# Plain products in the first two feed-forward blocks of a two-layer encoder

## Chip, cores, metric

One core of one Trainium2 chip runs the whole program. The metric is device time of one execution in microseconds (us).

## The reference, cut to what matters

Two layers work on a residual x of 1024 prompt and 64 sample rows, width 1024. Each layer is a mixer followed by a SwiGLU feed-forward, both behind an RMS norm with a shift and scale from a conditioning vector:

```python
def rms_norm(x, g):
    xf = x.astype(f32)
    return xf * lax.rsqrt(jnp.mean(xf * xf, -1, keepdims=True) + EPS) * g.astype(f32)
...
        hn = (rms_norm(x, norm_ffn[l]) * (1.0 + sc2) + sh2).astype(x.dtype)
        x = x + ((1.0 + g2) * swiglu(hn, ffn_wg[l], ffn_wu[l], ffn_wd[l])).astype(x.dtype)
```

swiglu is silu(hn times gate matrix) times (hn times up matrix), times the down matrix; the hidden width D_FF is 2816, that is 22 blocks of 128.

## The kernel before

x lies transposed in eight tiles of 128 x 1088 (features by rows). Every fp32 product is three passes over operands that are split in a high part (a cast on ACT) and a low part (a subtraction on POOL or DVE, `split`, L98 and L99): high by high, high by low, low by high.

The up half of the feed-forward (`up_half`) goes over 22 blocks of 128 hidden features. The two matrices of a block (gate and up) and the two halves of the rows form a 2 x 2 problem, solved with seven products in place of eight. Each product is 2 x 12 matmuls of 272 columns, so a block has 168 matmuls, into four accumulators accX, accY, accZ, accW in PSUM. For this the normalised x is turned into seven operands (`ops`: some are x itself, some sums and differences of quarters of x), and the four weight quarters of a block into seven weights (`weights`, three of them sums), each split into wh (ACT) and wl (POOL) in rings of 5 buffers of 128 x 512.

The last out-projection of the mixer (`project`) goes over four chunks of 272 rows (CH4). After each chunk `enter` stores x to DRAM, takes the norm's sums (L223), the power -1/2 on POOL (L232), spreads it over the partitions by a matmul (L239), copies it to SBUF (L374), multiplies x by it (L376), applies scale and shift (L379), and after every second chunk makes the first four operands (`first_ops`). `late_ops` makes the other three at the start of `up_half`. Block 0 needs the first operands of both halves.

The down half (`down_half`) multiplies 22 hidden blocks, parked in DRAM (hid_dram), by w_down in eight groups of two or three blocks. x is loaded back from DRAM ahead of it (`unpark`). In layer 0 the conditioning of layer 1 is worked out during the down half: `ada_tick` is called after each of the 24 chunks of a group and does two or three column blocks, each two dot products (L191 to L194) on DVE, or one on DVE and one on POOL with ACT.

A scheduler writes each engine's instruction list out ahead of time; at run time each engine goes through its list in order. Pools hand out buffers in turn, and whoever takes a buffer waits for its last reader.

Of the kernel before, what the change touches and what calls it, by code (L numbers as in the profile page):

```python
# [21 lines left out]
KD = 8  # L22
# [32 lines left out]
def hybrid_encoder(ctx: ExitStack, tc: tile.TileContext, I, O):  # L55
# [20 lines left out]
    def soon():  # L76
        return tc.high_priority(offset=SOON)
# [7 lines left out]
    def psum_pool(name):  # L85
        stack = ExitStack()
        stage["psum"] = stack.enter_context(tc.tile_pool(name=name, bufs=1, space=bass.MemoryType.PSUM,
                                                         reuse_waits="tile"))
        return stack
# [235 lines left out]
    def split_at(src, dst, j, lo_eng):  # L325
        c = slice(j * Q, (j + 1) * Q)
        split(src, dst[:, 0, c], dst[:, 1, c], lo_eng)
# [4 lines left out]
    def enter(l, x, tag, stat_tmp, tmp):  # L332


        ops = [[] for _ in range(7)]

        def late_ops(j):
            A, B = slice(j * Q, (j + 1) * Q), slice(HT + j * Q, HT + (j + 1) * Q)
            for k in range(4):
                split_at(x[k + 4][:, A], ops[4][k], j, G)  # L340
            for k in range(4):
                V.tensor_sub(x[k + 4][:, A], x[k + 4][:, A], x[k][:, A])
                split_at(x[k + 4][:, A], ops[5][k], j, V)
            for k in range(4):
                d, c = x[k + 4][:, B], slice(j * Q, (j + 1) * Q)
                hi, lo = ops[6][k][:, 0, c], ops[6][k][:, 1, c]
                S.activation(hi, d, AF.Copy, scale=-1.0)
                V.scalar_tensor_tensor(lo, d, -1.0, hi.bitcast(F32), ALU.mult, ALU.subtract)

        def first_ops(j):  # L350
            A, B = slice(j * Q, (j + 1) * Q), slice(HT + j * Q, HT + (j + 1) * Q)
            if j == 0:
                for o, t in ((0, tag), (1, tag), (2, "C"), (3, "C")):
                    ops[o] = [halves(u(t, F32R, "op")) for _ in range(4)]
            for k in range(4):
                split_at(x[k][:, A], ops[0][k], j, V)
            for k in range(4):
                a, b, d = x[k][:, A], x[k][:, B], x[k + 4][:, B]
                t1 = tmp()[:, :Q]
                V.tensor_sub(t1, b, a)  # L360
                V.tensor_sub(b, b, d)
                V.tensor_sub(a, a, b)
                split_at(a, ops[1][k], j, V)
                split_at(b, ops[2][k], j, G)
                split_at(t1, ops[3][k], j, G)

        def after(ci):
            c0, n = CH4[ci]
            r = slice(c0, c0 + n)
            for k in range(KD):  # L370
                dma(x_dram[k][:, r], x[k][:, r])
            rs = norm_stats(CH4[ci], x, stat_tmp)
            kept = tmp()[:, :n]
            S.copy(kept, rs)  # L374
            for k in range(KD):
                (G if k in (2, 3, 7) else V).tensor_mul(x[k][:, r], x[k][:, r], kept)  # L376
                for r0, rn, b in rng(c0, n):
                    v = x[k][:, r0:r0 + rn]
# [4 lines left out]
        return (ops, late_ops), after  # L383

    def up_half(l, ops_late, t_tag, op_tag):
        ops, late_ops = ops_late
        with phase_pool(f"up{l}") as fp:
            layout(fp, ("n22", NT, 4), ("t4", NT, 4), ("b21", NT, 4), ("wg", 1024, 2), ("wu", 1024, 2), ("s1", 512, 1),
                   ("wh", 512, 5), ("wl", 512, 5))

            def w_split(src):
                hi = fp.tile([P, 512], F32R, name="wh", tag="wh", bufs=5)
                lo = fp.tile([P, 512], F32R, name="wl", tag="wl", bufs=5)
                split(src, hi, lo, G)
                return hi, lo

            def weights(f):
# [3 lines left out]
                dma(wu, I["wu"][l, f])  # L401
                s1 = fp.tile([P, 512], F32, name="s1", tag="s1", bufs=1)
                w11, w12, w21, w22 = wg[:, :512], wg[:, 512:], wu[:, :512], wu[:, 512:]
                with soon():
                    yield w_split(w11)
                    V.tensor_add(s1, w21, w22)
                    V.tensor_add(w21, w11, w21)
                    V.tensor_add(w11, s1, w11)
                    yield w_split(w11)
                    yield w_split(w21)  # L410
                    yield w_split(s1)
                    yield w_split(w12)
                    V.tensor_add(w12, w11, w12)  # L413
                    yield w_split(w22)
                    yield w_split(w12)

            with soon():
                for o, tag in ((4, "b21"), (5, "t4"), (6, "n22")):
                    ops[o] = [halves(fp.tile([P, NT], F32R, name="op", tag=tag, bufs=4)) for _ in range(4)]
                late_ops(0)  # L420
                late_ops(1)
            stage["open"].close()
            with psum_pool(f"acc{l}"):
                ap = stage["psum"]

# [9 lines left out]
                for f in range(FF):  # L435
                    X, Y, Z, W = (ap.tile([P, 2, 512], F32, name="acc" + n, tag="acc" + n, bufs=1) for n in "XYZW")
# [33 lines left out]
                    for part in ((steps[:4], steps[4:]) if f == 0 else [[st] for st in steps]):  # L470
                        wt = [next(ws) for _ in part]
                        for j in range(2):
                            for w, (acc, op, start, use) in zip(wt, part):
                                product(acc, w, op, j, start)
                                if j == 1:
                                    with soon():
                                        use()
# [13 lines left out]
    def down_half(l, x, fp, t_tag, after=None, last=None, tick=None):  # L491
        f = 0
        for gi, size in enumerate(GROUPS):
            hs, ws = [], []
            for f in range(f, f + size):
# [11 lines left out]
            f += 1  # L507
            if gi == len(GROUPS) - 1 and last:
                last(ws, hs)
            else:  # L510
                project(ws, hs, x, mod(l, 5), after if gi == len(GROUPS) - 1 else tick, ("t", "z", "mm"))

# [7 lines left out]
    with phase_pool("wp") as stage["w"], phase_pool("mix") as mp:  # L520
# [474 lines left out]
        def out_group(g, after=None, chunks=CH):  # L995
# [13 lines left out]
            project(ws, hs, x, mod(0, 2), after, ("t", "z") if after else ("mm", "mm"), chunks)  # L1009
# [40 lines left out]
        ops, after = enter(0, x, "A", slots(mp, "kv", 3, 2, 4), slots(mp, "wt", 2, 2, 3))  # L1050
# [27 lines left out]
    up_half(0, ops, "B", "A")  # L1078
    with phase_pool("ffn0") as fp:
# [3 lines left out]
        x = unpark("A")  # L1083
# [5 lines left out]
        def ada_tick(ci):  # L1089
            with later():  # L1090
                for n in range(3 if len(todo) > 24 else 2):
                    if not todo:
# [5 lines left out]
                             lambda: fp.tile([P, 1024], BF16, name="junk", tag="junk"), j % 2 == 0)  # L1098
# [3 lines left out]
        box2, after = norm_into(1, 0, "B", "C", x, ntmp, ntmp)  # L1102
        with later():
            decay_consts()
        down_half(0, x, fp, "B", after, tick=ada_tick)
# [3 lines left out]
    h = box2[0]  # L1109
    with phase_pool("odd") as gp, phase_pool("w2") as w2, phase_pool("wp2") as stage["w"]:  # L1110
# [99 lines left out]
        def odd_out(js, own, aft=None, chunks=CH):  # L1210
# [15 lines left out]
            project(ws, hs, x, mod(1, 2), aft, ("t", "z", "mm"), chunks)  # L1226
# [3 lines left out]
        ops, after = enter(1, x, "B", slots(gp, "un", 12, 2, 4, Q), slots(gp, "un", 12, 2, 4, Q))  # L1230
# [41 lines left out]
    up_half(1, ops, "A", "B")  # L1272
    with phase_pool("ffn1") as fp:
# [4 lines left out]
        def finish(ws, hs):  # L1278
# [116 lines left out]
        x = unpark("B")  # L1395
        down_half(1, x, fp, "A", last=finish)
# [75 lines left out]
```

## Time and profile before

| | before |
|---|---|
| median of three runs | 2861.4 us (2857.73 to 2866.29) |
| the profiled execution's own time | 2864.79 us |
| its span | 2863.0 us |
| mean granted TensorE clock | 0.946 |
| busy: PE, DVE, ACT, POOL | 2610.7, 1814.2, 1026.6, 1269.6 us |

The span is what the profile covers; the execution's own time is 1.8 us longer. PE is TensorE's matmuls, PEld its weight loads, SPq a DMA issue on SyncE. A busy share of PE counts overlapped matmuls once.

### The profile page before, as it was taken

Reading aid. Unit: us, or ns where it says so; the run is one execution under the profiler, and the core shown is the slowest. Engines: PE = TensorE matmul, PEld = TensorE weight load, DVE = VectorE, ACT = ScalarE, POOL = GpSimd, SP = SyncE. Lnnn points to the kernel's source line nnn. Section 1 sums busy time; section 2 is a strip of 40 time slices with the busy share of each in tenths; the row PEclk is TensorE's granted clock in tenths of the full one; section 3 lists DMA queues with packets and bytes.
Section 4 is the critical chain, followed back from the end, with each engine's and each line's share of the span. In section 5 each row is a group of like instructions: output and inputs, shape, how many; then the busy total and the mean of one; then the engine's idle time right before and its main releaser. Section 6 shows DMA issues by size and latency. Waiting matters only on the chain.

```text
span 2863.0 us, 44449 instructions
## 1 busy us (share of the span) xinstructions
PE 2610.7 (91%) x17584; PEld 2549.8 (89%) x17584; DVE 1814.2 (63%) x2806; ACT 1026.6 (36%) x1891; POOL 1269.6 (44%) x923
## 2 busy tenths in 40 slices
PE   6898999999894999999799969998769999989998
PEld 6898989998783999999799969998669999989997
DVE  8778664568988343443788875668864344346555
ACT  3224343353555322222422155563442222232112
POOL 6546443355636444444443453344454444433222
PEclk9999988999996999999899979999889999999998
DMA  6232112112211222222854411221212222253211
GB/s 235 89 115 87 55 45 80 43 62 105 71 62 63 69 83 77 70 89 63 291 171 161 133 62 55 67 68 51 92 38 81 78 69 91 68 177 130 94 43 63
DMA packets 104561, 260.93 MB, mean 91 GB/s; under 512 B 17185, under 2 KB 42785, under 8 KB 104353
## 3 DMA queue, kind: packets, MB, share of 16 engines
q1 hardware_dynamic: 104352, 258.10, 27.7%
q8 instruction: 138, 2.26, 0.3%
q14 instruction: 71, 0.57, 0.1%
HBM read 207.36 MB, written 50.69 MB: 90 GB/s over the span
## 4 chain that ended last, share of the span: by engine, by line
PE 60%; DVE 22%; DMA 5%; ACT 5%; issue 4%; POOL 4%; SPq 0%; DVEq 0%; POOLq 0%; ACTq 0%
PE accZ L431 9%; PE accX L431 9%; PE accW L431 9%; PE ps_mm L127 7%; PE ps_mm L311 5%; PE accY L431 5%; PE ps_t L311 4%; PE ps_z L311 4%; DVE junk L194 3%; DVE x L316 3%; DVE xc L51 2%; DMA w_raw<-in_adaT 1%; DVE om L779 1%; PE ps_z L882 1%; PE ps_z L770 1%
## 5 line engine op out<-in xcount | busy, mean ns | idle before, releaser
L99 POOL TENSOR_TENSOR w_lo<-w_raw,w_hi 128x1024 fp32r<-128x1024 f32 x88 | 236.1, 2692 | 377.0 <-ACT w_hi L98 333.5
L99 POOL TENSOR_TENSOR wl<-wg,wh 128x512 fp32r<-128x512 f32 x176 | 228.3, 1297 | 225.8 <-ACT wh L98 225.1
L431 PE MATMUL accX<-op,wh 128*128 128x272 f32 x1408 | 275.0, 291 | 33.6 <-ACT wh L98 33.6
L446 DVE TENSOR_TENSOR tg<-accY,tg 128x544 f32<-128x544 f32 x44 | 31.9, 724 | 386.2 <-PE accY L431 364.9
L431 PE MATMUL accW<-op,wh 128*128 128x272 f32 x1408 | 274.4, 287 | 0.0
L431 PE MATMUL accZ<-op,wh 128*128 128x272 f32 x1408 | 271.1, 287 | 0.0
L431 PEld LDWEIGHTS accX<-op,wh 128*128 128x128 f32 x1408 | 224.1, 191 | 34.2 <-ACT wh L98 34.2
L127 PE MATMUL ps_mm<-h_hi,w_hi 128*128 128x384 f32 (+1 forms) x640 | 219.6, 343 | 11.2 <-ACT w_hi L98 9.9
L431 PEld LDWEIGHTS accW<-op,wh 128*128 128x128 f32 x1408 | 223.2, 188 | 0.4 <-ACT wh L98 0.4
L431 PEld LDWEIGHTS accZ<-op,wh 128*128 128x128 f32 x1408 | 220.8, 188 | 0.4 <-ACT wh L98 0.4
L127 PE MATMUL ps_mm<-h_hi,w_lo 128*128 128x384 f32 (+1 forms) x640 | 218.0, 342 | 2.0 <-POOL w_lo L99 2.0
L127 PE MATMUL ps_mm<-h_lo,w_hi 128*128 128x384 f32 (+1 forms) x640 | 217.7, 340 | 0.0
L431 PE MATMUL accX<-op,wl 128*128 128x272 f32 x704 | 204.9, 291 | 12.7 <-POOL wl L99 12.7
L98 ACT CAST wh<-wg 128x512 fp32r<-128x512 f32 x176 | 109.1, 621 | 283.8 <-DVE wg L413 142.4
L431 PE MATMUL accW<-op,wl 128*128 128x272 f32 x704 | 202.6, 288 | 0.0
L431 PE MATMUL accZ<-op,wl 128*128 128x272 f32 x704 | 202.4, 288 | 0.0
L98 ACT CAST w_hi<-w_raw 128x1024 fp32r<-128x1024 f32 x86 | 88.8, 1049 | 244.3 <-PE ps_mm L311 164.0
L316 DVE SCALAR_TENSOR_TENSOR x<-ps_mm,mods,x 128x384 f32<-128x384 f32 (+4 forms) x306 | 140.2, 482 | 51.1 <-PE ps_mm L311 50.8
L99 POOL TENSOR_TENSOR wl<-wu,wh 128x512 fp32r<-128x512 f32 x88 | 132.7, 1508 | 56.4 <-ACT wh L98 46.4
L99 POOL TENSOR_TENSOR wl<-s,wh 128x512 fp32r<-128x512 f32 x44 | 56.9, 1293 | 213.9 <-ACT wh L98 203.2
L431 PEld LDWEIGHTS accX<-op,wl 128*128 128x128 f32 x704 | 134.5, 191 | 13.4 <-POOL wl L99 13.4
L431 PE MATMUL accY<-op,wh 128*128 128x272 f32 x704 | 137.4, 288 | 1.6 <-ACT wh L98 1.6
(464 smaller groups left out, 7992.7 us busy)
## 6 DMA issues: line engine op xcount, KB each, us to landing
ada_raw<-in_adaT SPq DMA_DIRECT2D x48, 512.0 KB, 3.5
hid_dram<-hid SPq DMA_DIRECT2D x88, 272.0 KB, 3.9
wg<-in_wg SPq DMA_DIRECT2D x44, 512.0 KB, 4.2
wu<-in_wu SPq DMA_DIRECT2D x44, 512.0 KB, 3.6
w_raw<-in_wd SPq DMA_DIRECT2D x44, 512.0 KB, 4.4
hid_lo<-hid_dram SPq DMA_DIRECT2D x40, 544.0 KB, 6.0
w_raw<-in_w_in_even SPq DMA_DIRECT2D x28, 512.0 KB, 3.6
w_raw<-in_adaT SPq DMA_DIRECT2D x24, 512.0 KB, 3.6
```

The source lines that it names most:

```text
L51: return lambda *a, **k: self.tc.keep_in_program_order(f(*a, **k))
L98: S.copy(hi, src)
L99: (lo_eng or G).tensor_sub(lo, src, hi.bitcast(F32))
L127: PE.matmul(ps[:, :n], a[:, k * P:(k + 1) * P], b[:, c0:c0 + n], start=(i == 0), stop=(i == last))
L194: V.scalar_tensor_tensor(junk(), raw, 1.0, cb[v], ALU.mult, ALU.mult, accum_out=mods[l][:, t, v:v + 1])
L311: PE.matmul(ps[:, :n], a[:, m * P:(m + 1) * P], b[:, c0:c0 + n], start=(i == 0), stop=(i == 3 * nk - 1))
L316: V.scalar_tensor_tensor(x[m][:, r0:r0 + rn], ps[:, r0 - c0:r0 - c0 + rn], gate[:, m, b:b + 1], x[m][:, r0:r0 + rn], ALU.mult, ALU.add)
L431: PE.matmul(acc[:, j, :Q], a[:, k * P:(k + 1) * P], op[k][:, b, c], start=(start == 1 and i == 0), stop=(i == 11), skip_group_check=True)
L446: V.tensor_sub(t, y_, t)
L770: PE.matmul(z[:M, :bn], qs[:, j, s * P:s * P + M], ks[:, k0 + b0:k0 + b0 + bn], start=(j == 0), stop=(j == 1))
L779: V.tensor_tensor_scan(om[:, 0:d][:, ::-1], om[:, 0:d][:, ::-1], om[:, 0:d][:, ::-1], om[:, d:d + 1], ALU.mult, ALU.bypass)
L882: PE.matmul(ps[:L, a, :L // 2], K[:, c0:c0 + L], q, start=True, stop=True)
```

## The change

- Blocks 0 and 1 of each layer take plain products (`plain_block`): per chunk of 272 rows two outputs of 24 matmuls, 192 a block, on operands that `enter` now writes directly (B11, B12, B21, B22, by L351 to L353 of the new file, which read the spread norm from PSUM). Blocks 2 to 21 keep the seven products; their operands are made by `sums` between the two plain blocks in program order.
- The rings of wh and wl have 6 buffers in place of 5. One weight sum is taken with the other sign.
- The PSUM banks are laid out in a fixed order; the last out-projection uses banks t and mm.
- The loads of x stand behind the loads of the first down group in program order.
- `ada_tick` does three column blocks each time until all 48 are done (16 ticks; before 20, three for 8 ticks and two for 12). Of 48 column blocks 30 share with POOL and ACT in place of 24.

```diff
-            kept = tmp()[:, :n]
-            S.copy(kept, rs)
+            o = c0 % HT
             for k in range(KD):
-                (G if k in (2, 3, 7) else V).tensor_mul(x[k][:, r], x[k][:, r], kept)
+                t = B[(1, 0, 2, 3)[2 * (k // 4) + ci % 2]][k % 4]
                 for r0, rn, b in rng(c0, n):
...
-                    S.activation(v, v, AF.Identity, scale=scale[l][1][:, k, b:b + 1], bias=mods[l][:, 3 * KD + k, b:b + 1])
-            if ci % 2:
-                first_ops(ci // 2)
...
+                    V.scalar_tensor_tensor(v, v, A, rs[:, r0 - c0:r0 - c0 + rn], ALU.mult, ALU.mult)
+                    S.activation(hi, v, AF.Identity, bias=bias)
+                    V.scalar_tensor_tensor(lo, v, bias, hi.bitcast(F32), ALU.add, ALU.subtract)
...
-                   ("wh", 512, 5), ("wl", 512, 5))
+            layout(fp, ("t4", NT, 4), ("t1", NT, 4), ("t3", NT, 4), ("wg", 1024, 2), ("wu", 1024, 2), ("s1", 512, 1),
+                   ("wh", 512, 6), ("wl", 512, 6), ("hid0", NT, 2))
...
+            def sums():
...
+                for k in range(KD):
+                    for r0, rn, b in rng(0, NT):
+                        v = x[k][:, r0:r0 + rn]
+                        S.activation(v, v, AF.Identity, bias=mods[l][:, 3 * KD + k, b:b + 1])
...
+                for k in range(4):
+                    a, b, c, d = x[k][:, :HT], x[k][:, HT:], x[k + 4][:, :HT], x[k + 4][:, HT:]
+                    V.tensor_sub(d, b, d)
+                    V.tensor_sub(b, b, a)
+                    V.tensor_sub(a, a, d)
+                    V.tensor_sub(c, c, a)
+                    split(d, T3[k][:, 0, :], T3[k][:, 1, :], V)
+                    split(b, T1[k][:, 0, :], T1[k][:, 1, :], G)
+                    split(c, T4[k][:, 0, :], T4[k][:, 1, :], G)
...
+                return B11, T2, T3, T1, B21, T4, B22
...
+                def plain_block(f, order):
+                    hid = fp.tile([P, NT], F32, name="hid0", tag="hid0", bufs=2)
+                    with soon():
+                        ws = [w_split(w) for w in fetch(f)]
+                    for n, ci in zip("XYZW", order):
...
+                        for v in range(2):
+                            i = 0
+                            for hf in range(2):
+                                op = ((B11, B21), (B12, B22))[ci % 2][hf]
+                                w = ws[2 * v + hf]
...
+                            S.activation(h, acc[:, 0, :Q], AF.Silu)
+                            V.tensor_mul(h, h, acc[:, 1, :Q])
...
+                plain_block(0, range(4))
+                ops = sums()
+                plain_block(1, (1, 3, 0, 2))
+                for f in range(2, FF):
...
+        got = fetch(0)
+        x = unpark(x_tag)
...
-                for n in range(3 if len(todo) > 24 else 2):
+                for n in range(3):
...
-                             lambda: fp.tile([P, 1024], BF16, name="junk", tag="junk"), j % 2 == 0)
+                             lambda: fp.tile([P, 1024], BF16, name="junk", tag="junk"), j % 3 != 0)
```

Three places of the instruction lists show where the change moves work. Numbers behind a name tell one buffer or tile from another; op is an operand, wh and wl a weight's high and low part.

First, PE where the up half of layer 0 begins. ps_o holds the norm's sums (L223, now L224) and its spread (L239, now L240) of chunks 2 and 3. Before:

```order
L223 MATMUL ps_o_8255<-ones_66,ntmp_7831 128x1 x3
L239 MATMUL ps_o_8262<-ident_65,r1_8259 128x128 x3
L431 MATMUL accX_8422<-op_7984,wh_8433 128x272 x2
L431 MATMUL accX_8422<-op_7984,wl_8434 128x272
```

Now:

```order
L224 MATMUL ps_o_8234<-ones_66,ntmp_7851 128x1 x3
L240 MATMUL ps_o_8241<-ident_65,r1_8238 128x128 x3
L435 MATMUL accX_8338<-op_7823,wh_8322 128x272 x2
L435 MATMUL accX_8338<-op_7823,wl_8323 128x272
```

The first product still stands behind the spread of the last chunk, but its operand op_7823 is one of the second chunk's, and its weight is w11 as loaded.

Second, POOL ahead of the weights of the first blocks in layer 0. Before, block 0's first wl stands behind the 16 operand splits of half 0 and 1:

```order
L99 TENSOR_TENSOR op_8352<-x_5909,op_8352 128x272
L99 TENSOR_TENSOR op_8353<-x_5910,op_8353 128x272
L99 TENSOR_TENSOR wl_8434<-wg_8428,wh_8433 128x512
L99 TENSOR_TENSOR wl_8441<-wg_8428,wh_8440 128x512
```

Now (wl_8331 and wl_8335 are block 0's, wl_8629 to wl_8641 block 1's, wl_8861 block 2's):

```order
L100 TENSOR_TENSOR wl_8335<-wu_8319,wh_8334 128x512
L100 TENSOR_TENSOR wl_8629<-wg_8624,wh_8628 128x512
L100 TENSOR_TENSOR wl_8633<-wg_8624,wh_8632 128x512
L100 TENSOR_TENSOR op_8559<-x_5907,op_8559 128x544
L100 TENSOR_TENSOR op_8560<-x_5908,op_8560 128x544
L100 TENSOR_TENSOR op_8567<-x_5911,op_8567 128x544
L100 TENSOR_TENSOR op_8561<-x_5909,op_8561 128x544
L100 TENSOR_TENSOR op_8568<-x_5912,op_8568 128x544
L100 TENSOR_TENSOR op_8562<-x_5910,op_8562 128x544
L100 TENSOR_TENSOR op_8569<-x_5913,op_8569 128x544
L100 TENSOR_TENSOR wl_8637<-wu_8625,wh_8636 128x512
L100 TENSOR_TENSOR op_8570<-x_5914,op_8570 128x544
```

Block 0's weights now stand ahead of all operand splits; the third weight of block 1 stands behind seven of them.

Third, PE in a seven-product block in mid-layer, at the second product into accX and accZ. Before:

```order
L431 MATMUL accW_10432<-op_8359,wh_10620 128x272
L431 MATMUL accX_10652<-op_8350,wh_10782 128x272 x2
L431 MATMUL accW_10432<-op_8359,wh_10620 128x272
L431 MATMUL accW_10432<-op_8359,wl_10621 128x272
L431 MATMUL accW_10432<-op_8360,wh_10620 128x272 x2
L431 MATMUL accW_10432<-op_8360,wl_10621 128x272
L431 MATMUL accW_10432<-op_8361,wh_10620 128x272 x2
L431 MATMUL accW_10432<-op_8361,wl_10621 128x272
L431 MATMUL accX_10652<-op_8350,wl_10783 128x272
```

Now:

```order
L449 MATMUL accZ_10635<-op_8566,wh_10705 128x272 x2
L449 MATMUL accZ_10635<-op_8566,wl_10706 128x272
L449 MATMUL accW_10190<-op_8560,wh_10288 128x272
L449 MATMUL accW_10190<-op_8560,wl_10289 128x272
L449 MATMUL accW_10190<-op_8561,wh_10288 128x272 x2
L449 MATMUL accW_10190<-op_8561,wl_10289 128x272
L449 MATMUL accW_10190<-op_8562,wh_10288 128x272 x2
L449 MATMUL accW_10190<-op_8562,wl_10289 128x272
L449 MATMUL accX_10633<-op_7827,wh_10763 128x272 x2
L449 MATMUL accZ_10635<-op_8567,wh_10793 128x272 x2
L449 MATMUL accX_10633<-op_7827,wl_10764 128x272
```

By the lists, wh_10763 goes into the buffer that wh_10705 leaves (the first row of this piece is its last reader), and wh_10793 into that of wh_10288, which accW of two blocks back still reads. Before, wh_10782 takes the buffer of a weight whose last matmul stands 26 matmuls ahead of its use.

## Rows read from the trace of the kernel before

**Rows 1.** The page: span, busy time by engine, chain that ended last.

```profile
span 2863.0 us, 44449 instructions
...
PE 2610.7 (91%) x17584; PEld 2549.8 (89%) x17584; DVE 1814.2 (63%) x2806; ACT 1026.6 (36%) x1891; POOL 1269.6 (44%) x923
...
PE 60%; DVE 22%; DMA 5%; ACT 5%; issue 4%; POOL 4%; SPq 0%; DVEq 0%; POOLq 0%; ACTq 0%
```

**Rows 2.** Windows: stretch, length, busy us by engine, granted clock, DMA.

```profile
940.00:1370.00 430.00, 430.00 (x3441) 430.00 (x3440) 182.46 (x226) 122.50 (x204) 191.79 (x143) 1.00 0.27 83
...
1400.00:1670.00 270.00, 260.63 (x1548) 256.92 (x1549) 241.44 (x419) 67.41 (x94) 120.80 (x52) 0.99 0.46 152
```

**Rows 3.** Windows of the transition into the up half, layer 0.

```profile
890.00:900.00 10.00, 0.00 (x0) 0.00 (x0) 9.86 (x19) 10.00 (x30) 5.66 (x7) 0.50 0.18 54
```

**Rows 4.** Timeline of PE there: start, us, operation, [idle before].

```profile
862.63 0.28 PE L311 MATMUL ps_z<-o_hi,w_lo 128*128 128x272 f32 x1
...
885.72 1.65 PE L239 MATMUL ps_o<-ident,r 128*128 128x128 f32 x6 [8.38 <-POOL r L232]
904.18 0.82 PE L431 MATMUL accX<-op,wh 128*128 128x272 f32 x2 [16.81 <-ACT wh L98]
911.38 0.59 PE L431 MATMUL accX<-op,wl 128*128 128x272 f32 x1 [6.37 <-POOL wl L99]
911.77 0.65 PE L431 MATMUL accX<-op,wh 128*128 128x272 f32 x2
```

**Rows 5.** Timeline of POOL there.

```profile
899.52 10.39 POOL L99 TENSOR_TENSOR op<-x,op 128x272 fp32r<-128x272 f32 x11
909.87 1.46 POOL L99 TENSOR_TENSOR wl<-wg,wh 128x512 fp32r<-128x512 f32 x1
```

**Rows 6.** Groups by form, 850 to 912 us: busy us, mean ns | idle before.

```profile
L99 POOL TENSOR_TENSOR op<-x,op 128x272 fp32r<-128x272 f32 x16 | 15.0, 959 | 0.0
...
L99 DVE TENSOR_TENSOR op<-x,op 128x272 fp32r<-128x272 f32 x16 | 11.1, 736 | 0.0
...
L259 DVE TENSOR_TENSOR ntmp<-ntmp 128x272 f32<-128x272 f32 x8 | 3.3, 428 | 0.0
...
L316 DVE SCALAR_TENSOR_TENSOR x<-ps_t,mods,x 128x272 f32<-128x272 f32 x3 | 1.5, 491 | 0.0
```

**Rows 7.** The chain of work, 938 to 1000 us: start, us, what.

```profile
948.49 3.01 PE accX L431 x24
```

**Rows 8.** Timeline in mid-layer, PE, ACT, POOL: one weight's hand-over.

```profile
1146.67 0.41 PE L431 MATMUL accX<-op,wh 128*128 128x272 f32 x2
...
1147.17 0.62 ACT L98 CAST wh<-s 128x512 fp32r<-128x512 f32 x1 [5.50 <-PE accX L431]
...
1147.87 1.29 POOL L99 TENSOR_TENSOR wl<-s,wh 128x512 fp32r<-128x512 f32 x1 [5.35 <-ACT wh L98]
```

**Rows 9.** The page's groups: weight loads of PE (mean ns).

```profile
L431 PEld LDWEIGHTS accX<-op,wh 128*128 128x128 f32 x1408 | 224.1, 191 | 34.2 <-ACT wh L98 34.2
```

**Rows 10.** Groups by form, 940 to 1370 us, DVE on accW.

```profile
L463 DVE TENSOR_TENSOR tg<-accW,tg 128x544 f32<-128x544 f32 x21 | 14.9, 711 | 0.0
```

**Rows 11.** Timelines, end of the up half: PE of both layers.

```profile
1377.36 0.29 PE L431 MATMUL accW<-op,wl 128*128 128x272 f32 x1
1390.31 0.69 PE L311 MATMUL ps_t<-hid_hi,w_hi 128*128 128x384 f32 x1 [12.66 <-ACT w_hi L98]
...
2575.81 0.69 PE L311 MATMUL ps_t<-hid_hi,w_hi 128*128 128x384 f32 x1 [10.46 <-ACT w_hi L98]
```

**Rows 12.** Timeline of SyncE's DMA issues, end of the up half, layer 0.

```profile
1380.49 0.87 SPq L183 DMA_DIRECT2D cbc<-in_cT  x2
```

**Rows 13.** The chain of work, layer 1: the weight's load.

```profile
2568.79 5.85 DMA w_raw<-in_wd
```

**Rows 14.** Groups by form, 1390 to 1680 us: the conditioning.

```profile
L194 DVE SCALAR_TENSOR_TENSOR junk<-ada_raw,cbc 128x1024 bf16<-128x1024 f32 x72 | 100.4, 1394 | 24.9 <-ACT junk L192 21.4 <-DMA ada_raw<-in_adaT 2.9
...
L191 POOL TENSOR_TENSOR ada_raw<-ada_raw,cbc 128x1024 f32<-128x1024 f32 x24 | 58.6, 2440 | 123.6 <-DVE junk L194 116.9 <-issue 6.7
```

More of the change, by code (lines that the diff above doesn't have):

```diff
@@ L83, in hybrid_encoder, with psum_pool @@
     stage = {}
-    def psum_pool(name):
+    def psum_pool(name, *banks):
         stack = ExitStack()
@@ L88, in psum_pool @@
                                                          reuse_waits="tile"))
+        layout(stage["psum"], *(banks or [(tag, 512, 2) for tag in ("z", "mm", "t", "o")]))
         return stack
@@ L319, in project, with enter @@
                 after(ci)
-    def split_at(src, dst, j, lo_eng):
-        c = slice(j * Q, (j + 1) * Q)
-        split(src, dst[:, 0, c], dst[:, 1, c], lo_eng)
     def halves(t):
         return t.rearrange("p (a t) -> p a t", a=2)
[L332 to L365, printed above, removed]
+    def enter(l, x, tag, stat_tmp):
+        B = []
         def after(ci):
@@ L369, in after @@
             r = slice(c0, c0 + n)
+            if not B:
+                B.extend([halves(u(t, F32R, "op")) for _ in range(4)] for t in (tag, tag, "C", "C"))
             for k in range(KD):
@@ L469, in up_half @@
                     ws = weights(f)
-                    for part in ((steps[:4], steps[4:]) if f == 0 else [[st] for st in steps]):
-                        wt = [next(ws) for _ in part]
+                    for acc, op, start, use in steps:
+                        w = next(ws)
                         for j in range(2):
[L473 to L477, printed above, removed]
+                            product(acc, w, op, j, start)
+                        with soon():
+                            use()
                     for _ in ws:
@@ L489, in hybrid_encoder, with down_half, fetch @@
     GROUPS = (2, 3, 3, 3, 3, 3, 3, 2)
-    def down_half(l, x, fp, t_tag, after=None, last=None, tick=None):
-        f = 0
-        for gi, size in enumerate(GROUPS):
+    def down_half(l, fp, x_tag, t_tag, use):
+        first = [sum(GROUPS[:gi]) for gi in range(len(GROUPS))]
+        def fetch(gi):
             hs, ws = [], []
-            for f in range(f, f + size):
+            for f in range(first[gi], first[gi] + GROUPS[gi]):
                 if gi == len(GROUPS) - 1:
@@ L506, in down_half @@
                 ws.append(load_w(I["wd"][l, f], fp, "wd", bufs=6))
-            f += 1
+            return ws, hs
+        got = fetch(0)
+        x = unpark(x_tag)
+        tick, after, last = use(x)
+        for gi in range(len(GROUPS)):
+            ws, hs = got if gi == 0 else fetch(gi)
             if gi == len(GROUPS) - 1 and last:
@@ L1008, in out_group @@
                 ws.append(load_w(I["w_out_even"][kt], lo_eng=V if g>-1 else None))
-            project(ws, hs, x, mod(0, 2), after, ("t", "z") if after else ("mm", "mm"), chunks)
+            project(ws, hs, x, mod(0, 2), after, ("t", "mm") if after else ("mm", "mm"), chunks)
         OUT_AT = ((2, 1, 2), (2, 1, 4), (3, 0, 3))
@@ L1049, in hybrid_encoder @@
         attn_o(*pend)
-        ops, after = enter(0, x, "A", slots(mp, "kv", 3, 2, 4), slots(mp, "wt", 2, 2, 3))
+        plain, after = enter(0, x, "A", slots(mp, "kv", 3, 2, 4))
         out_group(3, after, CH4)
@@ L1225, in odd_out @@
                     ws.append(load_w(I["w_out_odd"][j], w2 if own == "wd" else None, own, raw))
-            project(ws, hs, x, mod(1, 2), aft, ("t", "z", "mm"), chunks)
+            project(ws, hs, x, mod(1, 2), aft, ("t", "mm") if aft else ("t", "z", "mm"), chunks)
         KEPT = (0, 1, 2, 3, 4, 5)
         outs = {}
-        ops, after = enter(1, x, "B", slots(gp, "un", 12, 2, 4, Q), slots(gp, "un", 12, 2, 4, Q))
+        plain, after = enter(1, x, "B", slots(gp, "un", 12, 2, 4, Q))
         ts_ = [{} for _ in range(KD)]
@@ L1269, in hybrid_encoder @@
         dma(O["lrus"], lrus)
-    up_half(1, ops, "A", "B")
+    up_half(1, plain, "A", "B")
     with phase_pool("ffn1") as fp:
```

72 lines of the change are left out of this document (45 added, 27 removed).

## The prediction

> **What bounds the kernel now.** The page comes first: PE is busy 91% of the span and holds 60% of the chain that ended last; DVE has 22% of it [rows 1]. So PE's work counts one to one where PE is full, and the rest must be looked for where it is not. The windows say where that is. From 940 to 1370 us, most of the up half of layer 0, PE is busy 430.00 us of 430.00 at full clock [rows 2]: nothing is waited for there, 24 matmuls of 272 columns take 3.0 us [rows 7], 0.125 us each, and a seven-product block of 168 takes 21.0 us. The down half is nearly full as well (260.6 of 270 us), with DVE busy 241 us [rows 2]: DVE has little to spare there. The holes are at the two ends of the up half. The timeline of PE shows the first: the last projection matmul runs at 862.63, the spread of the last chunk's norm at 885.72, after 8.38 us of waiting for POOL, the first two products at 904.18 and the third only at 911.38, held by wh and then by wl [rows 4]. For 10 us in between PE does nothing and its granted clock is 0.50, the 1.2 GHz level [rows 3]. What holds wl is POOL's list: eleven operand splits up to 909.87, and wl behind them [rows 5]. The second hole is 12.66 us in layer 0, from the last product (1377.36) to the first down matmul (1390.31), and 10.46 us in layer 1 [rows 11]. The end of the up half of layer 0, less 22 blocks of 21.0 us, is 1377.65 - 462.0 = 915.65: as if the blocks had begun at full speed there. Layer 1 has the same pattern: its up half ends at 2575.81 - 10.46 = 2565.35 [rows 11], 1187.7 us later, and I take one working for both.
>
> **The earlier start: -27 us a layer.** Removed ahead of the first product are the copies of the spread, the multiplies by it, and all operand splits: 16 on POOL (0.959 us) and 16 on DVE (0.736) for one form alone [rows 6]. Added are one DVE operation per tile and chunk that reads the spread from PSUM, which I price as the PSUM evacuation at 0.491, and one that subtracts the high part, priced between 0.428 (POOL quiet) and 0.736 (POOL busy) [rows 6]. But the list keeps the last chunk's spread ahead of the first product, and DVE runs 16 of the new operations and 14 subtractions in among the evacuations of the last two chunks: 16 x 0.49 + 14 x 0.43 = 14 us, about what the multiplies took there. So the spread does not come much earlier. It ended at 887.4; POOL, which it waited for 8.38 us, is now nearly empty at that point, and I take 886 for the first product (884 to 889). The clock is at 0.50 then as before, so the first 24 matmuls run at 0.22 in place of 0.12 us (two overlapping ones take 0.65 us in rows 4, 0.41 in rows 8), which costs 2.4 us. As a start at full speed this is 888.4, 27.2 us before 915.65. The weights must be there too: their six splits are now ahead of everything on POOL, and 1.46 us [rows 5] each keeps ahead of 24 slow matmuls.
>
> **Two plain blocks: +6 us a layer.** 192 matmuls in place of 168, twice: 48 x 0.125 us.
>
> **Block 1 waits for its third weight: +9 us a layer.** PE reaches it after 192 + 24 matmuls, at 888.4 + 27.0 = 915.4. Its buffer is free by then, but its low part stands behind seven operand splits on POOL. These need the sums on DVE, the sums need ACT's bias on x, and that needs the last chunk's operands: 32 DVE pieces at about 0.49 after 886, so 901. From there the lists hold 19 DVE operations of 544 columns (0.71 each by the 544-wide ones of rows 10) and 8 POOL splits (at least the 1.29 of 512 columns, rows 8) up to this weight: 13.5 and 10.4 us. If the two engines ran side by side, the weight would come at about 917 and PE would wait 1.5 us; if each waits for the other, at 925 and 9.5. The forms speak for the second: a subtraction with both inputs in SBUF takes 0.736 us on DVE beside the POOL splits and 0.428 where POOL is quiet [rows 6]. I take a wait of 8 us, and 1 us for the clock that falls in it. The Trainium skill, "SBUF — State Buffer", section "Who interferes with whom", says that a DVE instruction with two SBUF inputs and a GpSimd instruction that reads SBUF take turns at a shared port for the whole instruction; by it the wait would be the full 9.5 us, 1.5 us more a layer, and the longer DVE time in these forms agrees with it.
>
> **A wait in every seven-product block: +14 us a layer.** This speaks most against the change and stands in no line of the diff. The lists now run accW's products two blocks late, so their weights keep buffers of the ring, and the second weights of accX and accZ must take buffers that PE has only just left. In the third piece of the order above, the last reader of wh_10705 is followed by 13 matmuls before the one that needs wl_10764. Between the two lie a cast on ACT and a split on POOL. Their price stands in one hand-over [rows 8]: the last high matmul starts at 1146.80 (the second of two, 0.125 after 1146.67), the cast at 1147.17, the split at 1147.87, and it ends at 1149.16, 2.36 us after that matmul's start. Add 0.08 for the hand-over to PE (that from ACT to POOL: 1147.87 less 1147.79) and a weight load of 0.19 [rows 9], which is not hidden when PE waits: 2.63 us. In sequence the matmul would start 14 x 0.125 = 1.75 us after. PE waits 0.88 us. The pattern recurs in 16 of the 20 blocks: 14 us. The wait is on a loop from PE through ACT and POOL to PE, so that no slack saved earlier pays for it. The same count in the list of before leaves 26 matmuls, 3.25 us, ahead of a cast alone, and agrees with 430.00 of 430.00. Bounds: 0, if the weights come before PE needs them after all, to 20 us (all 20 blocks at 1.0).
>
> **The tail of the up half: +6 us a layer.** The last 96 matmuls are accW's of blocks 20 and 21, in four pieces of 24 with nothing between, and each piece needs a DVE operation on the piece before it: 0.37 from the last matmul's start to DVE (as to ACT in rows 8), 0.71 [rows 10], 0.08, 0.19, less 0.125: 1.2 us, four times 5. Splits of loaded hidden blocks stand between these on DVE: 1 more (4 to 9 in all).
>
> **The start of the down half: -2.5 and -3.5 us.** In layer 0 the loads of the conditioning vectors go out at 1380.49 [rows 12], 9.8 us before the first down matmul [rows 11]. Now the second waits for the last product, 0.4 us after which it goes: 10.2 in place of 12.66. In layer 1 the weight's load goes out at 2568.79 [rows 13] and PE starts 7.0 us later [rows 11]; now it can go with the last product: 7.0 for 10.46. The loads of x hide behind products as before: by the lists 17 of 24 still stand ahead of the first hidden block.
>
> **The conditioning: +3 us, once.** Before, 72 DVE products at 1.394 and 24 POOL ones at 2.440 [rows 14], 159 us in 20 ticks; now 66 and 30, 165 us in 16. A tick has 11.2 us of PE (270 / 24) and its load rises from 8.0 to 10.3, beside everything else that DVE does. I take 3 (-4, since the last third of the down half is rid of it, to +12).
>
> **The sum.** Layer 0: -27.2 + 6 + 9 + 14 + 6 - 2.5 = +5.3; layer 1: +4.3; with the conditioning +12.6. The profiled execution's 2864.8 becomes 2877.4. That execution lies 3.4 us above the median of the runs, 2861.4, so the median becomes 2874. The fixed banks, the other sign of a sum and the sixth buffer cost nothing of their own: the sign is one DVE operation for another, with DVE busy 182 of 430 us there [rows 2].
>
> **Rivals.** What a measurement can tell from no change is 0.3%, 8.6 us either way (2852.8 to 2870.0).
>
> *Faster: the ring does not hold PE.* If the per-block wait is not there, 28 us go and the median is 2846. For it: PE never waited in 430 us with one buffer less. Against it: the durations of rows 8 hardly vary and leave no room. It decides the sign: faster needs the wait under some 0.2 us a block (3.5 us a layer), slower over some 0.75.
>
> *The same: the pieces cancel.* The wait is half as long (0.45 us, -14 us), or the wait of block 1 is 1.5 us in place of 9 (-15): 2859 to 2860. For it: the bounds of both terms. Against it: two terms would have to stay near their lower ends or one at it.
>
> *Slower still: DVE and POOL are late more often.* The first weight of each block has 22 matmuls, 2.75 us, for the same 2.63 us; a split that takes 0.3 us more beside a DVE operation costs 0.2 us in each of 40 blocks, 8 us, and with 9 us at each tail and 9 more in the conditioning the median is 2897. For it: wl's splits of 1.46 us [rows 5].
>
> **Chances and range.** The forecast 0.48 (2864 to 2884 by itself), faster 0.18, the same 0.22, slower still 0.12. The range 2848 to 2890 leaves out the outer half of the first and of the last, and the forecast's own tails. Below 2852.8 lies the first rival, 0.18; between the bounds the second and a fifth of the forecast, 0.32; above, 0.50.
>
> **What would show it.** In the new profile: the third plain matmul at about 886 in place of 911; PE idle for wl some 8 us in block 1, at 915 to 925; in mid-layer PE under 100% busy, with some 0.9 us per 21.9 us charged to wl or wh ahead of accX and accZ; four short waits for DVE ahead of accW at the end. If a window in mid-layer shows PE full, the fourth term is wrong and with it the sign; if the first product stands later than 895, the first is.

## The result, and the profile after

The changed kernel takes 2878.6 us (median of five runs, 2874.76 to 2879.69), the kernel before 2857.7 us (2855.15 to 2866.29): 1.0064 times as long, 95% interval 1.0046 to 1.0082. It is slower. The two profiled executions are 14.9 us apart (2879.69 and 2864.79 us); the ledger below is made between these two.

The page of the changed kernel first, the lines that answer to [rows 1]:

```profile
span 2877.9 us, 44436 instructions
...
PE 2643.8 (92%) x17680; PEld 2566.8 (89%) x17680; DVE 1813.5 (63%) x2806; ACT 1012.4 (35%) x1839; POOL 1221.1 (42%) x861
```

PE is busy 33 us more. 96 more matmuls make 12 us of that, and a busy PE here is also one at the lower clock or with its matmuls less overlapped, so the page alone does not tell where the time went. The timeline of PE in layer 0 does (answers to [rows 4]; start, us, operation, idle before it):

```profile
881.27 1.65 PE L240 MATMUL ps_o<-ident,r 128*128 128x128 f32 x6 [3.56 <-POOL r L233]
...
882.58 0.80 PE L435 MATMUL accX<-op,wh 128*128 128x272 f32 x2
883.18 0.43 PE L435 MATMUL accX<-op,wl 128*128 128x272 f32 x1
...
916.42 0.82 PE L435 MATMUL accX<-op,wh 128*128 128x272 f32 x2 [5.47 <-ACT wh L99]
923.29 0.59 PE L435 MATMUL accX<-op,wl 128*128 128x272 f32 x1 [6.05 <-POOL wl L100]
```

The third product runs at 883.18 in place of 911.38: the hole ahead of the up half is closed. Behind it there is a new one, from 910.95 to 923.29, in which block 1 waits for its third weight, first for the high part (two matmuls run at 916.42) and then for the low part. What POOL does in it:

```profile
906.95 15.07 POOL L100 TENSOR_TENSOR op<-x,op 128x544 fp32r<-128x544 f32 x7 [17.25 <-ACT op L99]
921.97 1.26 POOL L100 TENSOR_TENSOR wl<-wu,wh 128x512 fp32r<-128x512 f32 x1
923.19 1.34 POOL L100 TENSOR_TENSOR op<-x,op 128x544 fp32r<-128x544 f32 x1
```

Seven splits of operands, then the weight. In mid-layer, where PE had been busy 300.00 us of every 300 with 2402 matmuls before, the windows now say (columns as in [rows 2]):

```profile
1000.00:1300.00 300.00, 295.44 (x2316) 290.35 (x2315) 137.29 (x151) 82.41 (x138) 123.45 (x97) 1.00 0.23 75
```

86 matmuls fewer in 300 us, 10.7 us at 0.125. One such wait in the timeline of PE, ACT and POOL, the place of the third piece of the order:

```profile
1137.82 0.41 PE L449 MATMUL accZ<-op,wh 128*128 128x272 f32 x2
...
1138.32 0.62 ACT L99 CAST wh<-wg 128x512 fp32r<-128x512 f32 x1 [2.38 <-PE accZ L449]
...
1139.02 1.29 POOL L100 TENSOR_TENSOR wl<-wg,wh 128x512 fp32r<-128x512 f32 x1 [1.72 <-ACT wh L99]
...
1139.94 0.52 PE L449 MATMUL accZ<-op,wh 128*128 128x272 f32 x2 [0.33 <-ACT wh L99]
...
1140.36 0.40 PE L449 MATMUL accX<-op,wl 128*128 128x272 f32 x1
```

The last reader of the buffer starts at 1137.95, the cast at 1138.32, the split at 1139.02 and ends at 1140.31; the matmul that wants it starts at 1140.36, where 13 matmuls in sequence would have let it start at 1139.70. Note the bracket: it shows 0.33 us for accZ and nothing for accX, because the matmuls ahead are counted busy to their end. What a block really loses is read from its period: the same wait stands at 1139.94 and 1205.25, three blocks apart, 21.77 us a block in place of 21.0.

The end of the up half, both layers (answers to [rows 11]):

```profile
1367.42 0.52 PE L449 MATMUL accW<-op,wh 128*128 128x272 f32 x2 [0.83 <-DVE tg L484]
1374.36 0.82 PE L449 MATMUL accW<-op,wh 128*128 128x272 f32 x2 [3.68 <-DVE hid L473]
1380.99 0.52 PE L449 MATMUL accW<-op,wh 128*128 128x272 f32 x2 [0.82 <-DVE tg L484]
1385.17 0.49 PE L449 MATMUL accW<-op,wh 128*128 128x272 f32 x2 [0.91 <-DVE hid L473]
1399.00 0.69 PE L312 MATMUL ps_t<-hid_hi,w_hi 128*128 128x384 f32 x1 [10.60 <-ACT w_hi L99]
...
2595.09 0.54 PE L312 MATMUL ps_t<-hid_hi,w_hi 128*128 128x384 f32 x1 [4.99 <-ACT w_hi L99]
```

The four waits of the tail are there, the first down matmul stands 8.7 us later than before in layer 0 and 19.3 later in layer 1. From there to the end the changed kernel wins back 4.4 us (282.8 in place of 287.2).

### The profile page after: what moved, and what is told of

Read it like the earlier page. It is cut to its first block, busy times and chain, and to the rows that moved or that the text cites. A ratio compares the mean times of both kernels' runs of the same rounds, so it can differ in the third digit from the quotient of the medians.

```text
span 2877.9 us, 44436 instructions
## 1 busy us (share of the span) xinstructions
PE 2643.8 (92%) x17680; PEld 2566.8 (89%) x17680; DVE 1813.5 (63%) x2806; ACT 1012.4 (35%) x1839; POOL 1221.1 (42%) x861
## 5 line engine op out<-in xcount | busy, mean ns | idle before, releaser
L449 PE MATMUL accW<-op,wh 128*128 128x272 f32 x1280 | 259.1, 290 | 12.4 <-DVE hid L473 7.5
L449 PE MATMUL accZ<-op,wh 128*128 128x272 f32 x1280 | 248.3, 290 | 10.0 <-ACT wh L99 9.9
L449 PE MATMUL accX<-op,wh 128*128 128x272 f32 x1280 | 245.0, 288 | 0.0
L449 PEld LDWEIGHTS accW<-op,wh 128*128 128x128 f32 x1280 | 207.8, 191 | 14.2 <-DVE hid L473 6.1
L449 PEld LDWEIGHTS accZ<-op,wh 128*128 128x128 f32 x1280 | 200.3, 188 | 17.1 <-ACT wh L99 17.1
L449 PEld LDWEIGHTS accX<-op,wh 128*128 128x128 f32 x1280 | 200.4, 188 | 0.5 <-ACT wh L99 0.5
L449 PE MATMUL accX<-op,wl 128*128 128x272 f32 x640 | 187.4, 293 | 1.0 <-POOL wl L100 1.0
L449 PE MATMUL accW<-op,wl 128*128 128x272 f32 x640 | 186.0, 291 | 0.0
L449 PE MATMUL accZ<-op,wl 128*128 128x272 f32 x640 | 184.2, 288 | 0.0
L128 PEld LDWEIGHTS ps_mm<-h_hi,w_hi 128*128 128x128 f32 x640 | 126.0, 197 | 14.3 <-ACT w_hi L99 10.5
L317 DVE SCALAR_TENSOR_TENSOR x<-ps_t,mods,x 128x384 f32<-128x384 f32 (+3 forms) x220 | 106.8, 502 | 43.2 <-PE ps_t L312 43.0
L479 DVE TENSOR_TENSOR hid<-accZ,tg 128x544 f32<-128x544 f32 x40 | 29.0, 724 | 166.4 <-PE accZ L449 166.4
```

The costliest lines, as they stand in the source:

```text
L128: PE.matmul(ps[:, :n], a[:, k * P:(k + 1) * P], b[:, c0:c0 + n], start=(i == 0), stop=(i == last))
L317: V.scalar_tensor_tensor(x[m][:, r0:r0 + rn], ps[:, r0 - c0:r0 - c0 + rn], gate[:, m, b:b + 1], x[m][:, r0:r0 + rn], ALU.mult, ALU.add)
L449: PE.matmul(acc[:, j, :Q], a[:, k * P:(k + 1) * P], op[k][:, b, c], start=(start == 1 and i == 0), stop=(i == 11), skip_group_check=True)
L479: V.tensor_add(hA, z_, t)
```

## The experiments

**A sixth buffer, alone.** The kernel before, with one number changed.

```diff
-            layout(fp, ("n22", NT, 4), ("t4", NT, 4), ("b21", NT, 4), ("wg", 1024, 2), ("wu", 1024, 2), ("s1", 512, 1),
-                   ("wh", 512, 5), ("wl", 512, 5))
+                   ("wh", 512, 6), ("wl", 512, 6))
```

> The kernel before with one edit: the rings of wh and wl have 6 buffers in place of 5. My theory: the sixth buffer alone moves accW's products two blocks late in the written list, so that PE waits for the ACT cast and the POOL split of accX's and accZ's second weights in nearly every block (0.77 us each, 20 blocks, 15 us a layer) and four times for DVE at the end of each up half (7 us a layer): about 44 us slower, 2902 us; mid-layer PE below 100% busy, seven-product blocks 21.8 us apart. Rival: the late accW products come from the plain blocks or the fixed PSUM banks; then the sixth buffer changes nothing, 2858 us, and mid-layer PE stays full.

2897.3 us, 1.0145 (1.0130 to 1.0160). The windows in mid-layer and the waits of PE from 860 to 1420 us (in total, times, longest):

```profile
1000.00:1300.00 300.00, 295.35 (x2316) 290.39 (x2317) 139.17 (x151) 82.45 (x138) 124.37 (x97) 1.00 0.22 76
```

```profile
PE accZ L431 <- ACT wh L98: 5.6, 17, 0.3
PE accW L431 <- DVE tg L463: 5.1, 2, 4.3
```

The same 2316 matmuls in 300 us as in the changed kernel, and 39.6 us lost where 44 were expected. So the sixth buffer by itself is enough to make a list with these waits and the tail; the plain blocks and the banks are not needed for it. Whether they would be enough without it is a question for the run with five buffers below.

**Seven buffers.**

```diff
-                   ("wh", 512, 6), ("wl", 512, 6), ("hid0", NT, 2))
+                   ("wh", 512, 7), ("wl", 512, 7), ("hid0", NT, 1))
```

> The changed kernel with 7 buffers of wh and wl; to make room, the plain blocks share one hid0 buffer in place of two. My theory: the list of the blocks in mid-layer goes back to that of before, PE is full there (12 us less a layer), the four waits at the end become two (4 us less), and block 1 gets its third weight ahead of the operand splits but not its fourth (its wait 9 in place of 12 us): 38 us faster than the changed kernel, 2840 us. Rival: the waits in mid-layer come from ACT's and POOL's order or the port that POOL and DVE share, not from the ring; then PE still waits 0.3 us or more in each block there and the time stays within 8 us of 2879.

2843.7 us, 0.9952 (0.9936 to 0.9968): faster than both kernels. In mid-layer, and in the waits of PE around the up half of layer 0:

```profile
1000.00:1300.00 300.00, 300.00 (x2401) 300.00 (x2400) 129.18 (x161) 86.62 (x144) 135.73 (x101) 1.00 0.25 77
```

```profile
PE accX L435 <- POOL wl L100: 9.0, 1, 9.0
...
PE accW L449 <- DVE tg L484: 2.7, 1, 2.7
PE accX L449 <- DVE hid L441: 1.6, 1, 1.6
PE accW L449 <- DVE hid L473: 0.9, 1, 0.9
```

PE is full in mid-layer, and block 1's wait, now for its fourth weight, is 9.0 us, as expected. The gain over the changed kernel is 35 us, 38 were expected.

**The control for it: one hid0 buffer, six of wh and wl.**

```diff
-                   ("wh", 512, 6), ("wl", 512, 6), ("hid0", NT, 2))
+                   ("wh", 512, 6), ("wl", 512, 6), ("hid0", NT, 1))
```

> The changed kernel with one hid0 buffer for the plain blocks in place of two, six buffers of wh and wl as they are: the control of what seven buffers had to give up. My theory: the list in mid-layer and the wait of block 1 stay, within 3 us of the changed kernel's 2878.6. Rival: part of the gain of seven buffers came from hid0, and this one is faster by 5 us or more.

2876.7 us (2870.99 to 2879.46), 1.0053 (1.0036 to 1.0070), 2317 matmuls in 300 us of mid-layer: the gain of seven buffers is theirs.

**Eight buffers.** The plain blocks write hid0 chunk by chunk from one buffer of 272 columns, to make room.

```diff
-                   ("wh", 512, 6), ("wl", 512, 6), ("hid0", NT, 2))
+                   ("wh", 512, 8), ("wl", 512, 8), ("hid0", Q, 1))
...
-                        h = hid[:, c0:c0 + Q]
+                        h = fp.tile([P, Q], F32, name="hid0", tag="hid0", bufs=1)
...
-                    dma(hid_dram[f], hid)
+                            dma(hid_dram[f][:, c0:c0 + Q], h)
```

> The changed kernel with 8 buffers of wh and wl; to make room, the plain blocks write each chunk of hid0 from one buffer of 272 columns. My theory: all four weights of block 1 are split ahead of the operand splits, so that its wait goes (12 us less a layer); the waits for wh and wl in mid-layer go as well (12 us), but the list now has only two matmuls between a product into accZ and the DVE operation that frees it, so some 0.8 us are waited for DVE in each of 18 blocks (14 us a layer): 2840 to 2850 us, with PE waiting for DVE in mid-layer. Rival: the wait of block 1 is for the operands themselves, not for the place in POOL's list; then PE waits as long at 911 to 925 us.

2865.9 us, 1.0034 (1.0023 to 1.0046): 16 to 26 us more than expected. The waits of PE around the up half of layer 0:

```profile
PE accX L448 <- DVE hid L440: 14.3, 1, 14.3
...
PE accZ L448 <- DVE hid L469: 10.1, 18, 0.6
```

The second line is the DVE wait that was expected in 18 blocks. The first was not: block 1 runs through, and the wait moves to the start of block 2. PE wants accX of block 1 drained, and in DVE's list that stands behind L383, which waits 4.67 us for a wl of POOL, behind the drain of block 0's last chunk, which waits 2.35 us for ACT, and behind L381, which waits for a wl of POOL until 931.54. hid0's single small buffer, which each chunk must leave by DMA before the next is written, makes ACT wait 2.31 us there, but only until 931.28, so it is not what ended last. The wait is as long as the rival said, but PE waits for an accumulator and not for operands, and POOL's list still stands in the chain.

**The splits of the sums on DVE.**

```diff
-                    split(b, T1[k][:, 0, :], T1[k][:, 1, :], G)
-                    split(c, T4[k][:, 0, :], T4[k][:, 1, :], G)
+                    split(b, T1[k][:, 0, :], T1[k][:, 1, :], V)
+                    split(c, T4[k][:, 0, :], T4[k][:, 1, :], V)
```

> The changed kernel with the low parts of the eight sums b and c split on DVE in place of POOL. My theory: block 1 waits (12.3 us) because its weights stand behind these splits on POOL; with POOL free it waits some 3 us, for DVE, while the waits for wh and wl in mid-layer stay as they are (0.77 us a block): 9 us less a layer, 2860 us. Rival: the wait is for the sums as such (ACT's bias and DVE's subtractions, with 8 more operations now on DVE); then PE waits about as long at the same place for DVE and the time stays within 6 us of 2878.

2866.0 us, 1.0026 (1.0016 to 1.0036), 12.6 us less than the changed kernel where 18 were expected. Block 1 and the start of block 2 (L449) in the timeline of PE:

```profile
912.76 0.52 PE L435 MATMUL accX<-op,wh 128*128 128x272 f32 x2 [1.27 <-ACT wh L99]
915.10 0.40 PE L435 MATMUL accX<-op,wl 128*128 128x272 f32 x1 [1.82 <-POOL wl L100]
924.04 0.52 PE L449 MATMUL accX<-op,wh 128*128 128x272 f32 x2 [0.87 <-DVE hid L441]
```

4.0 us in three pieces in place of 11.5 idle in two. Most of the wait came from the splits on POOL ahead of the weight. The run takes away two things at once, the place in POOL's list and the time that POOL and DVE lose beside each other, so how the gain divides between them is not shown.

**Both, and the old conditioning with them.** Seven buffers with the splits on DVE, and the same with the old `ada_tick`.

> Seven buffers and the splits of the sums on DVE. My theory: the two gains add, mid-layer PE full and block 1 with some 3 us of wait: 7 us less a layer than seven buffers alone (2843.7), 2830 us. Rival: with POOL out of the way the block waits for DVE instead, as with eight buffers (14 us for the evacuation of a plain block's product); then 2843 us or more.

2838.3 us (2835.62 to 2840.84), 0.9929 (0.9913 to 0.9946), 8 us short of the expectation: the first product of block 2 now waits 5.5 us for DVE to drain block 1 (L441), the rival in part. The runs overlap those of seven buffers alone (2838.81 to 2847.59), so the totals leave open whether the second gain adds; the waits around block 1 in layer 0 fall from 10.8 to 6.9 us.

> As the last, with the conditioning as before the change (three a tick for 8 ticks, then two; every second one shared). My theory: the down half of layer 0 becomes 4 us shorter, as in the changed kernel (317.0 to 312.6 from its first matmul to the first product of the next mixer): 2826 us. Rival: the two ways of spreading do the same within the spread of runs, 2830 us.

2832.4 us, 0.9903 (0.9888 to 0.9918): the fastest of all, 26 us under the kernel before. The stretch named in the expectation takes 312.9 us, with the new conditioning 316.2.

**The old conditioning alone.**

```diff
-                for n in range(3):
+                for n in range(3 if len(todo) > 24 else 2):
...
-                             lambda: fp.tile([P, 1024], BF16, name="junk", tag="junk"), j % 3 != 0)
+                             lambda: fp.tile([P, 1024], BF16, name="junk", tag="junk"), j % 2 == 0)
```

> The changed kernel with the conditioning as before: three column blocks a tick for 8 ticks and two for 12, every second one shared with POOL. My theory: the down half of layer 0, from its first matmul to the first product of the next mixer, becomes some 3 us shorter (317.0 in the changed kernel, 313.9 before), nothing else moves: 2876 us. Rival: spreading helps by itself, and the 3 us come from the new start of that half; then it becomes longer by up to 4 us.

2874.1 us, 1.0055 (1.0034 to 1.0075); its runs overlap those of the changed kernel, so the totals do not decide. The stretch does: from the first down matmul (1402.88) to the first product of the next mixer (1715.51) it takes 312.6 us, the changed kernel 317.0 (1399.00 to 1715.98), the kernel before 313.9.

**Five buffers in the changed kernel, and seven in the one before.**

> The changed kernel with 5 buffers of wh and wl, as before the change. My theory: what counts is where the written list puts the second weights of accX and accZ, not that there are six; with five the list also takes buffers four and five matmuls after their last reader: 0.95 us in each of 20 blocks (7 us more a layer than now), block 1 waits for two weights in place of one: 2887 us. Rival: five buffers give back the list of before in mid-layer, as they did there: PE full, 12 us less a layer, 2855 us.

2886.1 us, 1.0095 (1.0080 to 1.0110), as expected. The windows in mid-layer:

```profile
1000.00:1300.00 300.00, 294.51 (x2295) 288.38 (x2293) 133.02 (x151) 80.85 (x137) 122.13 (x96) 1.00 0.21 72
```

So with five buffers the other parts of the change are enough for a list with waits, too. The ring's sixth buffer and the rest of the change each bring the waits by themselves, and neither alone accounts for them in the changed kernel.

> The kernel before with 7 buffers of wh and wl in place of 5. My theory: more buffers help or harm only through the written list. With seven, the list of the kernel before again takes buffers four and five matmuls after their last reader, as the changed kernel with five does (0.95 us in some 17 blocks, 16 us a layer), and waits at the end of the up half: 35 us slower, 2893 us. Rival: seven are enough for any list, as they were in the changed kernel: mid-layer PE full and 2858 us.

2895.4 us, 1.0131 (1.0110 to 1.0152), and the windows:

```profile
1000.00:1300.00 300.00, 294.91 (x2307) 289.46 (x2305) 129.26 (x151) 81.63 (x138) 122.12 (x96) 1.00 0.22 73
```

| buffers of wh and wl | kernel before | changed kernel |
|---|---|---|
| 5 | 2857.7 us, 2402 matmuls in 300 us | 2886.1 us, 2295 |
| 6 | 2897.3 us, 2316 | 2878.6 us, 2316 |
| 7 | 2895.4 us, 2307 | 2843.7 us, 2401 |
| 8 | not tried | 2865.9 us, 2308 |

More buffers are not better or worse as such: among these sizes a full PE goes with one list in each kernel, and one buffer more or less gives another list. The timelines of PE from 1100 to 1148 us show it. The two full kernels run their products in one and the same order (24 matmuls of accX, 10 of accY, 9 of accZ, 16 of accW, 2 of accX, 8 of accW, 3 of accX, 24 of accZ, and so on), both kernels with six in a second one, and the two that are slow with five and with seven in nearly a third. With eight the mid-layer waits are for DVE, not for weights.

## Why the prediction was right, term by term

The forecast was slower, for the reason that it put in the fourth term: the per-block wait. One sentence of its sum was wrong, that the sixth buffer costs nothing of its own. In the kernel before it costs 39.6 us, in the changed kernel it saves 7.5. The working had seen the late accW products in the lists, but held that they stand in no line of the diff, where the ring's size is one. The fixed banks and the other sign were not run alone; with both of them and seven buffers mid-layer PE is full. The ledger of layer 0, forecast and measured:

| term | forecast | measured |
|---|---|---|
| earlier start | -27.2 us | -31.8 |
| two plain blocks | +6.0 | +6.0 (matmul counts) |
| block 1's wait | +9 | +13.6 |
| wait in every seven-product block | +14 | +12.3 |
| tail of accW | +6 | +9.8 |
| start of the down half | -2.5 | -2.1 |
| sum of the terms | +5.3 | +7.8 |
| first down matmul | +5.3 | +8.7 (0.9 not assigned) |

Start: PE was done with the products ahead of block 1's third weight at 910.95 (916.42 less 5.47), so that the next matmul in sequence would have started at 910.8; less 216 matmuls of 0.125 us that is a start at 883.8, 31.8 us ahead of 915.65. The first product came at 882.58, not at 886: the spread of the last chunk waited 3.56 us for POOL in place of 8.38, with the power at 1.04 us. The slow matmuls behind it cost 1.2 us in place of 2.4: the granted clock was 0.50 up to 884.80 and 0.83 from there to 886.00, and 11 matmuls were slow, not 24. The working had no row that showed a quiet POOL there, and I took the gain too small.

Block 1: 12.2 us to the matmul at 923.29 and 1.4 more after it, with the matmuls slow at first (the first 12, from 923.29 to 926.18, took 2.89 us in place of 1.5, at a granted clock of 0.50). That is 4.6 us more than forecast, and it is the same 4.6 us by which the start came earlier. The working put the weight at 923.4 (PE there at 915.4, and a wait of 8), and the weight was used at 923.29; but PE reached it at 910.8. The two terms were not independent: as long as the weight comes last, time saved ahead of it turns into wait.

That the weight came when it was forecast is in part luck. The working gave a POOL split of 544 columns the 1.29 us of 512, 10.4 us up to the weight, and POOL took 16.3 (906.95 to 923.23). Against that, nine of DVE's twenty operations were done when POOL began, so that the two engines' times did not add up as in the bound of 925. The seven splits of 15.07 us are not alike; single lines of POOL and DVE:

```profile
906.95 5.88 POOL L100 TENSOR_TENSOR op<-x,op 128x544 fp32r<-128x544 f32 x1 [17.25 <-ACT op L99]
...
910.92 0.71 DVE L100 TENSOR_TENSOR op<-x,op 128x544 fp32r<-128x544 f32 x1
911.55 0.43 DVE L441 TENSOR_TENSOR hid<-hid,accY 128x272 f32<-128x272 f32 x1
911.90 1.50 DVE L404 TENSOR_TENSOR x<-x 128x544 f32<-128x544 f32 x1
912.79 1.80 POOL L100 TENSOR_TENSOR op<-x,op 128x544 fp32r<-128x544 f32 x1
913.33 1.84 DVE L405 TENSOR_TENSOR x<-x 128x544 f32<-128x544 f32 x1
...
919.40 1.33 POOL L100 TENSOR_TENSOR op<-x,op 128x544 fp32r<-128x544 f32 x1
```

The first took 5.88 us, while DVE ran eight subtractions with both inputs in SBUF one behind the other at 0.72 us; it ended 1.28 us after the start of L441, which has one input in PSUM. The next three took 1.80 to 1.82 while three subtractions on DVE took 1.50, 1.84 and 1.51. The last three, with DVE waiting or in L441, took 1.33, and the eighth 1.34. The first split is as long in layer 1 (5.88) and with seven and eight buffers (5.29 and 5.93). The Trainium skill ("SBUF — State Buffer", section "Who interferes with whom") says that a DVE instruction with two SBUF inputs contends with a GpSimd instruction that reads SBUF. The trace agrees with it: 5.88, 1.82 and 1.33 us for the same split on POOL, 0.72 and 1.84 for the same subtraction on DVE. In the experiment with the splits on DVE 7.5 of the 11.5 us idle go.

The wait in every block: 0.77 us measured (21.77 a block) and 0.88 forecast, in 16 blocks. Layer 0 has 15 such waits ahead of accZ and two of 0.24 and 0.28 us ahead of accX; the count of matmuls from 926.18 to 1365.81, 3414 in 439.63 us, gives 12.9 us for all of them, near the 12.3 of the table. The loop from the last reader to the next matmul took 2.41 us in place of 2.63: 0.27 had been added for the hand-over to PE and the weight load, while the matmul started 0.05 us after the split's end. By that the wait would be 0.66; the other 0.11 of the period is not assigned. The deciding point named in the rivals was 0.75 us, just below what was measured. That such a wait can be read from lists, before any trace of it, was borne out three times more: with six and seven buffers in the kernel before and five in the changed one.

The tail: 9.8 us (96 matmuls from 1367.42 to 1388.24 take 20.8 us in place of 12.0, and about 1.0 ahead of the first). One of the four waits was 3.68 us, since DVE stood at a split of a loaded hidden block that waited 2.54 us for its cast, and the cast waited 4.06 us for the block's load. The 24 matmuls behind this wait ran at a granted clock of 0.50, in 5.6 us in place of 3.0. These 2.6 us, which the term had not counted, are most of the 3.8 that it was short; the four waits themselves cost 7.0 us where 5 and 1 were forecast. In layer 1 two of them were 1.98 and 2.43.

The conditioning: forecast +3; 317.0 less 313.9 is +3.1, and the old conditioning in the changed kernel makes it 4.4. Layer 1: the first down matmul moved by another 7.5 us beyond what layer 0 had handed on (19.28 less 11.73), where the forecast had 4.3, by the same terms. Then the sum has a term that was missing: the down half of layer 1 took 4.4 us less. It falls into its first 60 us, in which the changed kernel runs 349 matmuls and the one before 322; after 280 us the counts are 1651 and 1650. The granted clock there is 0.83 in place of 0.69 in the first 10 us, but only one matmul more runs in these, and 1.00 in place of 0.84 in the third 10; PE waits 0.8 us for DVE in place of 1.9. How the 4.4 us divide between clock and waits was not tested.

The sum came out near, +14.9 us between the profiled executions and +12.6 forecast. The start and block 1 cancel by their cause; that the longer tail and the shorter down half of layer 1 nearly cancel is luck. The medians differ by 20.9: the profiled execution of before is among the slower of its kernel, 7.1 us above the median of 2857.7, where the forecast had taken off 3.4.

## What to carry to other kernels

Where lists are written ahead, read in them how many matmuls stand between the last reader of a buffer and the first use of what goes into it, and set that against the measured hand-over through the engines between: 13 matmuls of 0.125 us against 2.4 us of cast and split cost 12 us a layer, and this can be counted before anything runs. Where two engines reach the same point, work out when each gets there: the last 4.6 us that PE gained ahead of block 1 it lost again in waiting for a weight that came no earlier. A ring's size is to be measured together with the list that it makes, number by number: five buffers were the best in one kernel here and the worst in the other, seven the best in one and, level with six, the worst in the other. Work that is moved off the first product's path (here the operands of the seven products) must also stand behind the next weights in every list that it shares with them.

## What the runs showed of the hardware

A wait ahead of a matmul is largely hidden in the profile's idle times: 0.33 us were shown per block and 0.77 lost. The count of matmuls in a window, or the weight loads' busy time (290.35 us of 300), shows the loss; PE's busy time (295.44) shows less than half of it.

A mean can hide two engines holding each other up: the seven operand splits on POOL, 2.15 us each in the mean, were one of 5.88, three of 1.8 and three of 1.33, by what DVE did beside them.
